# Additions by DMA held from the start, sums of x in five steps, and five raw weight buffers instead of six

## The chip, the cores and the metric

The kernel runs on one core of a Trainium2 chip. Its time is the device time of one execution in microseconds (us). A core has five engines with a queue of instructions each: PE (TensorE, matmuls; PEld is its weight load), DVE (VectorE), ACT (ScalarE), POOL (GpSimd) and SP (SyncE, which here only issues DMAs). Each engine runs its own queue in order.

## The reference

A bidirectional encoder trunk of two layers over x of 256 tokens by 1024, in float32, with FF = 2816:

```python
def rms_norm(x, g):
    return x * rsqrt(mean(x * x, axis=-1) + 1e-6) * g

def swiglu(h, w_gate, w_up, w_down):
    return (silu(h @ w_gate) * (h @ w_up)) @ w_down

for l in range(2):
    x = x + 0.5 * swiglu(rms_norm(x, ffn1_norm[l]), ffn1_w_gate[l], ffn1_w_up[l], ffn1_w_down[l])
    h = rms_norm(x, mix_norm[l])
    qa, ka, va, qb, kb, vb = split(h @ w_in[l])
    # windowed attention with sinks (a) and differential attention (b)
    x = x + concat(oA, oB) @ w_out[l]
    x = x + 0.5 * swiglu(rms_norm(x, ffn2_norm[l]), ffn2_w_gate[l], ffn2_w_up[l], ffn2_w_down[l])
out = rms_norm(x, final_norm)
```

The change touches the four FFNs (two in each layer) and the norm ahead of each. The attention between them is called mix below.

## The kernel before

**Weights.** All weights are read once from HBM, 200 MB in all, in steps of 1 MB: a step is a tile of 128 partitions with 8 KB each, called raw (N_RAW = 6 of them). To reach float32 accuracy, each raw half is split in two parts: ACT casts it to the matmul's type (the high half), DVE subtracts that from the raw values (the low half). Both lie in 4 KB tiles called w from the pool s4 (N_S4 = 28). A product takes three matmuls, high by high, low by high, high by low. The same is done with x and with the hidden part h, whose transposes on PE give hT.

**The planner.** `specs` is a list of Steps in the order of use. `weights()` takes the next step for PE and calls `ahead(n)`, which issues, up to a point n counted in half steps, the splits, the preparations of a step (`prep`) and the loads. n is `look[0]` half steps ahead of the step in use: IN_FFN = 8 in most FFNs, IN_MIX = 6 in the first FFN and in mix. `Split.part` calls `ahead` again when PE comes to the second half of a step. A load is issued when fewer than N_RAW raws are held; a raw is given back when its last split has been issued. The instructions stay in the order in which the program issues them on PE, ACT, DVE and POOL. Nothing is ordered by times.

**Groups.** An FFN goes through FF in five groups of 512 columns and a tail of 256. A group has gate and up products (x by 1024 rows of weights) and the down product of the group before, whose steps are down0 and down1 (two halves of the columns of D).

**Groups by seven** (`seven`, `by_seven`; the table SEVEN: groups 2 to 4 in the first FFN, 1 to 4 in the three others). Here the eight quarter products of a group's gate and up are replaced by seven, in the manner of a fast matrix multiplication, with sums of weights and sums of x. Four loads serve one group: a (gate, first half of the rows), b (up, first half), c (up, second half), d (gate, second half). Two sums of weights are formed by DMA: `gather(c, b)` reads c from HBM again and adds it onto b in SBUF, `gather(b, a)` adds b onto a. These are the additions of this document; POOL's queue issues them. Two more sums come from DVE: `plus(c, a)` and `plus(d, a)`, two instructions each, after which c, and then a and d, are free. From group 2 on, the steps in PE's order are: a, b+c, d, c, down0, a+b, a+b+c, a+b+c+d, down1. In group 1 of the later FFNs they are: a, d, down0, c, b+c, and then the same.

**Sums of x.** `make_sums` is a generator. It forms four combinations of the quarters of x with DVE, casts each on ACT and subtracts on DVE (three tiles with tag q and one with tag v). The FFN's code advances it by `next(sums)` at given points.

**Holding additions.** `issue` puts an addition on a list and lets it go at once, unless `hold` is set; `flush` clears `hold` and issues what has gathered, last in first out. Before, `hold` starts as False. `ffn_end` sets it, at the end of an FFN, and `Norm.stats` calls `flush` after it has computed r = (mean square + eps)^-0.5 on POOL. `stats` runs at the end of `take_x` (the first FFN's start) and in `Residual.late` (the others). In `take_x` it is followed by `constants()`, which puts ten or so small loads and operations for the attention on POOL's queue.

Of the kernel before, what the change touches and what calls it, by code (L numbers as in the profile page):

```python
# [12 lines left out]
ALU = mybir.AluOpType  # L13
# [8 lines left out]
NGRP = FF // 512  # L22
# [3 lines left out]
BIG = 1e33  # L26

AHEAD = 10
N_RAW, N_S4 = 6, 28
IN_FFN, IN_MIX = 8, 6  # L30
SEVEN = ((2, 3, 4), (1, 2, 3, 4))

# [2 lines left out]
def trunk(ctx: ExitStack, tc: tile.TileContext, x, n1, g1, u1, d1, nm, w_in, sink,  # L35
# [123 lines left out]
            issue(s.behind)  # L159


    pending, hold = [], [False]

    def issue(add):
        pending.append(add)
# [3 lines left out]
    def flush():  # L169
        hold[0] = False  # L170
        while pending:
            pending.pop(0)()
# [50 lines left out]
    look = [IN_MIX]  # L223
# [23 lines left out]
    def weights(less=0, held=False):  # L247

        i = at["use"]
        at["use"] += 1  # L250
        if i > 1:
            ahead(2 * i + look[0] - less)
        w = loaded[i]
        w.held = held
        return w
# [48 lines left out]
    class Norm:  # L304
# [42 lines left out]
        def make_sums(self):  # L347

            self.sm = []

            (t0, t1), (b0, b1) = [(t[:, :, 0:P], t[:, :, P:S]) for t in self.xg]

            def make(x, y, op):
                v = tmp().rearrange("p a (c s) -> p (a c) s", c=2)
                dve.tensor_tensor(v, x, y, op=op)
                tag, n = ("q", 3) if len(self.sm) < 3 else ("v", 1)
                sm = tp.tile([P, 2, 512], F32R, tag=tag, bufs=n, name=nm_(tag)).rearrange("p a (c s) -> p (a c) s", c=2)
                act.copy(sm[:, :, 0:P], v)
                self.sm.append(sm)
                return v  # L360

            def low(i, v):
                dve.tensor_tensor(self.sm[i][:, :, P:S], v, f(self.sm[i][:, :, 0:P]), op=ALU.subtract)

            s1 = make(b1, t1, ALU.subtract)
            s2 = make(s1, t0, ALU.add)
            low(0, s1)
            yield
            b0_ = make(b0, s2, ALU.subtract)
            low(1, s2)  # L370
            yield
            v = make(t1, t0, ALU.subtract)
            low(2, b0_)
            yield
            low(3, v)
            yield

# [10 lines left out]
        def stats(self, n=512):  # L388
            ms = tmp("ms", 2, (P, 2))
            dve.tensor_reduce(ms, self.ss.rearrange("p t (h q) -> p t h q", q=n // 256)[:, :, :, 0],  # L390
                              axis=mybir.AxisListType.X, op=ALU.add)
            dve.tensor_scalar(ms, ms, 1.0 / D, EPS, op0=ALU.mult, op1=ALU.add)
            self.r = tmp("r", 2, (P, 2))
            pool.tensor_tensor(self.r, ms, mhalf[:, 0:2], op=ALU.pow)
            flush()
            self.hr = tmp("hr", 2, (P, 2))
            dve.tensor_scalar_mul(self.hr, self.r, 0.5)

# [32 lines left out]
    def take_x(k):  # L431

        g, u = early
        if k == 0:
            for j in (0, 1):
                sl = norm.turn(j)
                next(g)
                norm.operands(j, sl)
                next(u)
        elif k == 1:  # L440
            for e in (g, u, g, u):
                next(e)
            norm.squares(0, 0, 512)
            norm.pair(2)
            norm.squares(1, 0, 512)
            ahead(5)
            norm.pair(3)
            norm.squares(0, 512, 512)
        elif k == 2:
            for e in early:  # L450
                next(e, None)
            ahead(7)
            norm.squares(1, 512, 512)
            norm.stats()
            constants()

    grow = const.tile([NG - 16, P], F32, name="grow")
    distB = const.tile([P, 2, S], F32, name="distB")
# [107 lines left out]
    class Residual:  # L566
# [14 lines left out]
        def late(self, k):  # L581

            if k == 1:
                self.nxt.pair(2)
                self.nxt.pair(3)
                self.squares(1)
            elif k == 2:
                self.nxt.stats()

    def ffn(norm, aside=None, before=None, final=False, sevens=SEVEN[1]):  # L590
        def silu(out_, acc, t):
# [3 lines left out]
        def gate(gs):  # L595
            g = []
            for t in range(2):
                n = gs[t].shape[1]
                g.append(silu(tmp().rearrange("p a n -> p (a n)")[:, :n], gs[t], t))
            return g  # L600
# [5 lines left out]
        def hidden(g, us):  # L606
            h = blk(F32)
            for t in range(2):
                up(h, us[t], g[t], t)
            return h  # L610

        def prod(xo, w):
            acc = bank()
            for k in range(4):
                hi, lo = w.part(k)
                xh, xl = xo(k)
                pe.matmul(acc, lhsT=xh, rhs=hi, start=k == 0, stop=False)
                pe.matmul(acc, lhsT=xl, rhs=hi, start=False, stop=False)
                pe.matmul(acc, lhsT=xh, rhs=lo, start=False, stop=k == 3)
            return acc  # L620

        def by_seven(h, g, sums):


            flat = lambda: tmp().rearrange("p a n -> p (a n)")

            def put(o, x, y, op):
                dve.tensor_tensor(o, x, y, op=op)
                return o

            m1, m7 = flat(), flat()
            if g > 1:
                act.copy(m1, prod(norm.quarter(0, 0), weights()))
                act.copy(m7, prod(norm.summed(3), weights(held=True)))
                hT = turn(h, 2)
                p2 = prod(norm.quarter(0, 1), weights())
                g0 = put(flat(), p2, m1, ALU.add)
                p3 = prod(norm.summed(2), weights())
                silu(g0, g0, 0)
                down(hT, g - 1, 0, weights())  # L640
            else:
                w = weights()
                next(sums, None)
                p1 = prod(norm.quarter(0, 0), w)
                hT = turn(h, (0,))
                w = weights()
                next(sums, None)
                act.copy(m1, p1)
                p2 = prod(norm.quarter(0, 1), w)
                hT += turn(h, (1,))  # L650
                w = weights()
                next(sums, None)
                g0 = put(flat(), p2, m1, ALU.add)
                silu(g0, g0, 0)
                down(hT, 0, 0, w)
                p3 = prod(norm.summed(2), weights())
                act.copy(m7, prod(norm.summed(3), weights()))
            h = blk(F32)
            p5 = prod(norm.summed(0), weights())
            late = g == max(sevens)  # L660
            p6 = prod(norm.summed(1), weights(look[0] - 5 if late else 0, late))
            u2 = put(flat(), p6, m1, ALU.subtract)
            u3 = put(m7, m7, u2, ALU.add)
            p4 = prod(norm.quarter(1, 1), weights(look[0] - 4 if late else 0, late))
            g1 = put(m1, p4, u3, ALU.subtract)
            w = weights(look[0] - 3 if late else 0)
            silu(g1, g1, 1)
            put(u3, u3, p5, ALU.subtract)
            put(u2, u2, p5, ALU.subtract)
            put(u2, u2, p3, ALU.add)  # L670
            up(h, u2, g0, 0)
            up(h, u3, g1, 1)
            down(hT, g - 1, 1, w)
            return h
# [19 lines left out]
        gs, us = [bank(), bank()], [bank(), bank()]  # L694
        if before is None:
            before = norm.late
        look[0] = IN_FFN - (1 in sevens)
        before(0)
        ws = (weights(), weights(2))
        for k in (0, 2):  # L700
# [7 lines left out]
        if 1 in sevens:  # L708
            norm.copies()
            sums = norm.make_sums()  # L710
        tokens(gs, norm.xs, w, 4)
        g = gate(gs)
        w = weights()
        next(sums, None)
        tokens(us, norm.xs, w, 4)
        h = hidden(g, us)
        for n in range(1, NGRP):
            if n in sevens:
                look[0] = IN_FFN + min(sevens) - n if before is not take_x else IN_MIX - (n == NGRP - 1)
                h = by_seven(h, n, sums)  # L720
                continue
            sums = norm.make_sums()
            gs = [bank(), bank()]
            tokens(gs, norm.xs, weights(), 0)
            hT = turn(h, 2)
            norm.copies()
            tokens(gs, norm.xs, weights(), 4)
            g = gate(gs)
            next(sums, None)
            us = [bank(), bank()]  # L730
            for k0 in (0, 4):
                tokens(us, norm.xs, weights(), k0)
                next(sums, None)
            h = hidden(g, us)
            for hh in range(2):
                down(hT, n - 1, hh, weights())
                if hh == 0:
                    next(sums, None)

        gu = [bank(), bank()]  # L740
        tokens(gu, norm.xs, weights(), 0)
# [390 lines left out]
```

## Time and profile before

| | us |
|---|---|
| median of 3 runs | 968.45 (966.74 to 970.66) |
| the profiled execution | 967.48 |
| its span in the trace | 965.7 |
| PE busy | 921.3 (95%) |
| DVE busy | 808.3 (84%) |
| ACT busy | 590.8 (61%) |
| POOL busy | 64.9 (7%) |

The FFNs' starts are at about 0, 316, 503 and 787 us (where the norm's r is made, or x is read). A row of a timeline reads: start, duration, engine, line, operation, output <- inputs, sizes, and how many like it were merged; in brackets stands the idle time before it, and what ended that. Nearly all instructions carry line 50, that of the helper that issues them, so they are told apart by their tiles. A row of the view by windows reads: the stretch and its length, then the busy time of PE, PEld, DVE, ACT and POOL with the number of instructions, the granted clock of PE, the DMA share and GB/s. A row of DMA issues ends with the median time from issue to landing.

### The profile page before, as it was taken

The page shows a single profiled execution, that of the slowest core. Times are in us where ns is not written, and L with a number is a line of the kernel's source. Part 1 is how long each engine was busy: PE and PEld are TensorE (multiplying, and loading weights), DVE is VectorE, ACT ScalarE, POOL GpSimd, SP SyncE. Part 2 cuts the span into 40 slices and gives each one's busy share as a digit, 9 for nine tenths or more (in the row PEclk, how much of TensorE's full clock was granted, in tenths as well). Part 3 has the DMA queues.
Part 4 walks back from the last instruction along what each step waited for, and adds up shares of the span by engine and source line. Part 5 has one row for each costly group of instructions (what it writes and reads, how often), then busy time and mean ns, then how long its engine had stood idle before and what let it go on. Part 6 is the DMA issues. An engine that isn't in the chain of part 4 may idle for free.

```text
span 965.7 us, 12600 instructions
## 1 busy us (share of the span) xinstructions
PE 921.3 (95%) x4696; PEld 771.9 (80%) x4696; DVE 808.3 (84%) x1125; ACT 590.8 (61%) x917; POOL 64.9 (7%) x83
## 2 busy tenths in 40 slices
PE   8499999999999889999997999999999996999997
PEld 6388888899888668888885888888998884888886
DVE  6376999959885699999868999997798668999995
ACT  7464766548765665665674675665577484666661
POOL 0220010000010110010010010000001010010011
PEclk9799999999999989999998999999999998999999
DMA  9893997947424786897748977978472357798841
GB/s 337 265 235 114 281 275 224 297 120 213 137 92 172 172 238 168 268 286 248 274 139 193 278 226 222 262 253 257 111 239 89 131 145 195 228 273 207 260 151 44
DMA packets 114061, 200.87 MB, mean 208 GB/s; under 512 B 3662, under 2 KB 31376, under 8 KB 114000
## 3 DMA queue, kind: packets, MB, share of 16 engines
q1 hardware_dynamic: 96528, 166.74, 50.5%
q0 software_dynamic: 16096, 31.75, 18.7%
q10 hardware_dynamic: 1376, 1.57, 0.5%
q8 instruction: 37, 0.61, 0.2%
q14 instruction: 24, 0.20, 0.1%
HBM read 199.00 MB, written 1.05 MB: 207 GB/s over the span
## 4 chain that ended last, share of the span: by engine, by line
PE 83%; DVE 7%; DMA 4%; ACT 3%; issue 1%; POOL 0%; SPq 0%; ACTq 0%; POOLq 0%; DVEq 0%
PE ps L50 83%; DVE w L50 4%; ACT w L50 2%; DMA raw<-in_ffn_w_up_dram 1%; DMA raw<-in_ffn_w_gate_dram 1%; DVE tmp L50 1%; DVE s L50 1%; DVE raw L50 1%; DMA xk<-in_x_dram 1%; ACT tmp L50 1%; ACT L50 0%; ACT q L50 0%; ACT v L50 0%; POOL raw L50 0%; SPq L153 0%
## 5 line engine op out<-in xcount | busy, mean ns | idle before, releaser
L50 PE MATMUL ps<-w,s 128*128 128x512 f32 (+1 forms) x2574 | 614.2, 396 | 30.9 <-ACT tmp L50 13.1
L50 PEld LDWEIGHTS ps<-w,s 128*128 128x128 f32 x2574 | 484.5, 191 | 136.2 <-ACT tmp L50 14.3
L50 DVE TENSOR_TENSOR w<-raw,w 128x1024 fp32r<-128x1024 f32 (+1 forms) x458 | 484.0, 1100 | 56.3 <-ACT w L50 54.3
L50 ACT CAST w<-raw 128x1024 fp32r<-128x1024 f32 (+1 forms) x458 | 409.6, 952 | 102.9 <-DVE raw L50 86.2
L50 PE MATMUL ps<-w,q 128*128 128x512 f32 x540 | 127.7, 390 | 0.0
L50 PEld LDWEIGHTS ps<-w,q 128*128 128x128 f32 x540 | 101.9, 189 | 21.4
L50 PE MATMUL ps<-s,w 128*128 128x256 f32 x672 | 84.0, 285 | 0.0
L50 PEld LDWEIGHTS ps<-s,w 128*128 128x128 f32 x672 | 81.7, 192 | 1.1
L50 DVE TENSOR_TENSOR raw<-raw,raw 128x1024 f32<-128x1024 f32 x60 | 70.6, 1217 | 0.0
L50 POOL DMA_DIRECT2D raw<-in_ffn_w_up_dram x30 | 39.1, 1357 | 409.8 <-DVE w L50 138.2
L50 ACT ACTIVATE s<-ps,gcol 128x256 fp32r<-128x256 f32 (+1 forms) x80 | 31.4, 479 | 46.6 <-PE ps L50 45.0
L50 ACT ACTIVATE tmp<-tmp,r 128x512 f32<-128x512 f32 x30 | 21.7, 723 | 49.4 <-DVE tmp L50 49.4
L50 PE MATMUL ps<-ident,s 128*128 128x128 f32 x304 | 41.2, 274 | 2.7 <-DVE s L50 2.7
L50 PE MATMUL ps<-w,v 128*128 128x512 f32 x180 | 43.3, 389 | 0.0
L50 PEld LDWEIGHTS ps<-ident,s 128*128 128x128 f32 x304 | 35.1, 140 | 9.8 <-ACT w L50 2.9
L50 PEld LDWEIGHTS ps<-w,v 128*128 128x128 f32 x180 | 33.8, 188 | 7.0
L50 ACT COPY tmp<-ps 128x512 f32<-128x512 f32 x34 | 19.9, 585 | 31.8 <-PE ps L50 29.4
L50 ACT ACTIVATE s<-s,negm 128x256 f32<-128x256 f32 x64 | 31.9, 500 | 6.6 <-DVE negm L50 6.4
L50 DVE TENSOR_TENSOR s<-ps,s 128x512 fp32r<-128x512 f32 x44 | 28.7, 683 | 7.9 <-ACT s L50 7.9
L50 ACT CAST s<-ps 128x512 fp32r<-128x512 f32 x44 | 24.2, 592 | 18.1 <-PE ps L50 18.1
L50 DVE TENSOR_TENSOR tmp<-ps,tmp 128x512 f32<-128x512 f32 x49 | 33.4, 682 | 1.6 <-PE ps L50 1.6
L50 ACT CAST q<-tmp 128x512 fp32r<-128x512 f32 x20 | 12.4, 621 | 34.7 <-DVE tmp L50 34.3
(106 smaller groups left out, 417.6 us busy)
## 6 DMA issues: line engine op xcount, KB each, us to landing
raw<-in_ffn_w_down_dram SPq DMA_DIRECT2D x44, 1024.0 KB, 6.4
raw<-in_ffn_w_gate_dram SPq DMA_DIRECT2D x39, 1024.0 KB, 8.6
raw<-in_ffn_w_up_dram SPq DMA_DIRECT2D x39, 1024.0 KB, 5.1
raw<-in_ffn_w_up_dram POOLq DMA_DIRECT2D x30, 1024.0 KB, 10.3
raw<-in_w_in_dram SPq DMA_DIRECT2D x14, 1024.0 KB, 5.6
raw<-in_ffn_w_gate_dram SPq DMA_DIRECT2D x8, 512.0 KB, 6.7
raw<-in_ffn_w_up_dram SPq DMA_DIRECT2D x8, 512.0 KB, 7.6
raw<-in_w_in_dram SPq DMA_DIRECT2D x8, 512.0 KB, 5.7
```

The lines of the kernel that those rows point to most:

```text
L50: ins = issue(*a, **k)
```

## The change

Three things are changed together. Additions by DMA are held from the beginning of the program, and `flush` is called by the callers of `stats`: in `take_x` behind `constants()`, in `Residual.late` right behind `stats`. `make_sums` yields after each group of DVE additions and after each group of casts, five times instead of four, with two casts in one step, and the places of its `next` calls move with it. The raw buffers are five instead of six, and the 8 KB go to two more tiles of the pool s4, with which the splits in FFNs that begin with a group by seven run one half step further ahead. In group 1 of these FFNs the `weights()` calls stand at slightly other places.

```diff
@@ -26,7 +26,7 @@
 BIG = 1e33
 
 AHEAD = 10
-N_RAW, N_S4 = 6, 28
+N_RAW, N_S4 = 5, 30
 IN_FFN, IN_MIX = 8, 6
 SEVEN = ((2, 3, 4), (1, 2, 3, 4))
 
@@ -159,7 +159,7 @@
             issue(s.behind)
 
 
-    pending, hold = [], [False]
+    pending, hold = [], [True]
 
     def issue(add):
         pending.append(add)
@@ -350,28 +350,35 @@
 
             (t0, t1), (b0, b1) = [(t[:, :, 0:P], t[:, :, P:S]) for t in self.xg]
 
-            def make(x, y, op):
+            def add(x, y, op):
                 v = tmp().rearrange("p a (c s) -> p (a c) s", c=2)
                 dve.tensor_tensor(v, x, y, op=op)
+                return v
+
+            def high(v):
                 tag, n = ("q", 3) if len(self.sm) < 3 else ("v", 1)
                 sm = tp.tile([P, 2, 512], F32R, tag=tag, bufs=n, name=nm_(tag)).rearrange("p a (c s) -> p (a c) s", c=2)
                 act.copy(sm[:, :, 0:P], v)
                 self.sm.append(sm)
-                return v
 
             def low(i, v):
                 dve.tensor_tensor(self.sm[i][:, :, P:S], v, f(self.sm[i][:, :, 0:P]), op=ALU.subtract)
 
-            s1 = make(b1, t1, ALU.subtract)
-            s2 = make(s1, t0, ALU.add)
+            s1 = add(b1, t1, ALU.subtract)
+            s2 = add(s1, t0, ALU.add)
+            yield
+            high(s1)
+            high(s2)
+            yield
             low(0, s1)
+            b0_ = add(b0, s2, ALU.subtract)
+            low(1, s2)
+            v = add(t1, t0, ALU.subtract)
             yield
-            b0_ = make(b0, s2, ALU.subtract)
-            low(1, s2)
+            high(b0_)
+            high(v)
             yield
-            v = make(t1, t0, ALU.subtract)
             low(2, b0_)
-            yield
             low(3, v)
             yield
 
@@ -392,7 +399,6 @@
             dve.tensor_scalar(ms, ms, 1.0 / D, EPS, op0=ALU.mult, op1=ALU.add)
             self.r = tmp("r", 2, (P, 2))
             pool.tensor_tensor(self.r, ms, mhalf[:, 0:2], op=ALU.pow)
-            flush()
             self.hr = tmp("hr", 2, (P, 2))
             dve.tensor_scalar_mul(self.hr, self.r, 0.5)
 
@@ -453,6 +459,7 @@
             norm.squares(1, 512, 512)
             norm.stats()
             constants()
+            flush()
 
     grow = const.tile([NG - 16, P], F32, name="grow")
     distB = const.tile([P, 2, S], F32, name="distB")
@@ -586,6 +593,7 @@
                 self.squares(1)
             elif k == 2:
                 self.nxt.stats()
+                flush()
 
     def ffn(norm, aside=None, before=None, final=False, sevens=SEVEN[1]):
         def silu(out_, acc, t):
@@ -639,17 +647,15 @@
                 silu(g0, g0, 0)
                 down(hT, g - 1, 0, weights())
             else:
+                p1 = prod(norm.quarter(0, 0), weights())
+                hT = turn(h, (0,))
+                next(sums, None)
                 w = weights()
-                next(sums, None)
-                p1 = prod(norm.quarter(0, 0), w)
-                hT = turn(h, (0,))
-                w = weights()
-                next(sums, None)
                 act.copy(m1, p1)
                 p2 = prod(norm.quarter(0, 1), w)
                 hT += turn(h, (1,))
+                next(sums, None)
                 w = weights()
-                next(sums, None)
                 g0 = put(flat(), p2, m1, ALU.add)
                 silu(g0, g0, 0)
                 down(hT, 0, 0, w)
@@ -694,7 +700,7 @@
         gs, us = [bank(), bank()], [bank(), bank()]
         if before is None:
             before = norm.late
-        look[0] = IN_FFN - (1 in sevens)
+        look[0] = IN_FFN
         before(0)
         ws = (weights(), weights(2))
         for k in (0, 2):
@@ -708,15 +714,21 @@
         if 1 in sevens:
             norm.copies()
             sums = norm.make_sums()
+            next(sums)
         tokens(gs, norm.xs, w, 4)
-        g = gate(gs)
-        w = weights()
+        if 1 in sevens:
+            w = weights()
+            g = gate(gs)
+        else:
+            g = gate(gs)
+            w = weights()
         next(sums, None)
         tokens(us, norm.xs, w, 4)
         h = hidden(g, us)
+        next(sums, None)
         for n in range(1, NGRP):
             if n in sevens:
-                look[0] = IN_FFN + min(sevens) - n if before is not take_x else IN_MIX - (n == NGRP - 1)
+                look[0] = IN_FFN + 1 + min(sevens) - n if before is not take_x else IN_MIX - (n == NGRP - 1)
                 h = by_seven(h, n, sums)
                 continue
             sums = norm.make_sums()
@@ -734,8 +746,7 @@
             h = hidden(g, us)
             for hh in range(2):
                 down(hT, n - 1, hh, weights())
-                if hh == 0:
-                    next(sums, None)
+                next(sums, None)
 
         gu = [bank(), bank()]
         tokens(gu, norm.xs, weights(), 0)
```

## The prediction

> **What bounds the kernel now.** I read the page's busy line first, then the windows by stage, then the timelines of single engines at the places that the change touches.
>
> ```profile
> PE 921.3 (95%) x4696; PEld 771.9 (80%) x4696; DVE 808.3 (84%) x1125; ACT 590.8 (61%) x917; POOL 64.9 (7%) x83
> ...
> 87.00:165.00 78.00, 77.56 (x351) 64.05 (x349) 77.13 (x80) 49.80 (x57) 5.14 (x4) 1.00 0.85 244
> 345.00:450.00 105.00, 105.00 (x470) 87.00 (x470) 100.50 (x103) 65.97 (x76) 6.42 (x5) 0.99 0.84 245
> 317.00:343.00 26.00, 19.42 (x77) 14.62 (x76) 19.30 (x22) 14.87 (x19) 2.56 (x2) 0.90 0.74 170
> ```
>
> Over the span PE is the bound, at 95%. But in the groups by seven (87 to 165 in the first FFN, 345 to 450 in the second) DVE is full too: 77.13 of 78.00 us and 100.50 of 105.00. The third line is the start of the second FFN, where neither is full. The end of the groups shows how much PE still lies behind DVE:
>
> ```profile
> 449.91 3.57 DVE L50 TENSOR_TENSOR w<-raw,w 128x1024 fp32r<-128x1024 f32 x3
> 450.94 2.24 PE L50 MATMUL ps<-w,s 128*128 128x512 f32 x9
> 164.91 3.47 PE L50 MATMUL ps<-w,s 128*128 128x512 f32 x14 [0.44 <-DVE w L50]
> ```
>
> The first of DVE's three low halves ends at about 451.1. PE's nine matmuls begin at 450.94, and the third of them, some 0.5 us later, is the first that takes that half. So the reserve there is 0.3 us, and at 164.91 PE already waits 0.44 for DVE. **What DVE loses inside the groups by seven, PE loses at their end.** The idle time of PE is at the start and in the three later FFN starts, shown below.
>
> **Part 1: the start.** Additions are held from the beginning and let go behind the constants. Before, the first addition stands ahead of r (the norm's reciprocal root) on POOL's queue.
>
> ```profile
> 27.20 0.17 DVE L50 TENSOR_SCALAR ms<-ms 128x2 f32<-128x2 f32 x1
> 29.43 1.28 ACT L50 ACT_TABLE_LOAD   x1
> 41.42 1.48 POOL L50 DMA_DIRECT2D raw<-in_ffn_w_up_dram  x1 [39.91 <-DMA raw<-in_ffn_w_up_dram]
> 42.43 1.25 POOL L50 TENSOR_TENSOR r<-ms,mhalf 128x2 f32<-128x2 f32 x1
> 43.71 1.27 ACT L50 ACTIVATE tmp<-ps,r 128x512 f32<-128x512 f32 x2 [12.99 <-POOL r L50]
> 44.45 7.14 PE L50 MATMUL ps<-w,s 128*128 128x512 f32 x24 [13.13 <-ACT tmp L50]
> 127.57 5.60 PE L50 MATMUL ps<-w,q 128*128 128x512 f32 x24
> ```
>
> The mean square is ready at 27.37, and r could follow at once (it lasts 1.25). POOL instead waits for the load that the addition adds onto, and makes r at 42.43. ACT's table load ends at 30.71 and silu needs some 0.7 more for PE's first bank, so PE can go on at 31.45, not 44.45: 13.0 us. PE's next 24 matmuls took 7.14 us, against 5.60 for 24 at 127.57; without the stall I take these 1.5 us back as well. Sum: −14.5.
>
> The addition now waits behind the constants on POOL, whose own waits for DMAs move with it:
>
> ```profile
> 59.82 0.50 POOL L50 TENSOR_TENSOR s<-s 128x128 f32<-128x128 f32 x1 [3.25 <-DMA s<-in_lam_k_dram]
> 84.96 1.04 PE L50 MATMUL ps<-ident,s 128*128 128x128 f32 x8
> ```
>
> From the end of r (43.68) to the end of the constants (60.32) pass 16.6 us before. After, r ends at about 28.7, so the constants end by 45.3, and the first addition lands by 45.3 + 11.3 = 56.6 (its time is priced below). DVE meets the sum's split ahead of the hidden part that PE transposes at 84.96, which is due at 84.96 − 14.5 = 70.5. With a pair of splits (2.35, as at 106.86), h and the small sums between, which I take as 4 us, it must be there at about 64. That is 7 us of cover, so I cost it at nothing; beyond it each us costs one.
>
> **Part 2: five raw buffers.** One buffer less makes each load wait for a later release. For mix, tails and down steps the loads land 7 us or more ahead of their first read, and a shift of one release costs nothing. One chain has no such room. In a group by seven, b of the next group is loaded, c is added onto it by a DMA on POOL's queue, and ACT and DVE split the sum.
>
> ```profile
> 89.00 0.37 SPq L153 DMA_DIRECT2D raw<-in_ffn_w_up_dram  x1
> 91.16 2.35 DVE L50 TENSOR_TENSOR raw<-raw,raw 128x1024 f32<-128x1024 f32 x2
> 94.61 1.29 POOL L50 DMA_DIRECT2D raw<-in_ffn_w_up_dram  x1 [28.06 <-DVE tmp L50]
> 106.86 2.35 DVE L50 TENSOR_TENSOR w<-raw,w 128x1024 fp32r<-128x1024 f32 x2
> ...
> 372.34 0.37 SPq L153 DMA_DIRECT2D raw<-in_ffn_w_up_dram  x1
> 377.07 2.35 DVE L50 TENSOR_TENSOR raw<-raw,raw 128x1024 f32<-128x1024 f32 x2
> 378.00 1.29 POOL L50 DMA_DIRECT2D raw<-in_ffn_w_up_dram  x1 [19.29 <-DMA raw<-in_ffn_w_up_dram]
> 386.19 6.90 DVE L50 TENSOR_TENSOR w<-raw,w 128x1024 fp32r<-128x1024 f32 x6 [0.34 <-ACT w L50]
> 409.72 2.35 DVE L50 TENSOR_TENSOR raw<-raw,raw 128x1024 f32<-128x1024 f32 x2
> 425.41 2.35 DVE L50 TENSOR_TENSOR w<-raw,w 128x1024 fp32r<-128x1024 f32 x2
> ```
>
> Before, the load of b starts at 89.00 and 372.34, as soon as the split of a down step has freed the sixth buffer. With five, that split frees a buffer that an earlier load already claims, and b waits for the next release, of c, by DVE's second addition: 91.16 + 2.35 = 93.51 in the first FFN, 379.42 and 412.07 in the second. DVE has a fixed amount of work from there to the first half of the sum: 106.86 − 93.51 = 13.35 us; 391.87 (the sixth of the x6 at 386.19) − 379.42 = 12.45; 425.41 − 412.07 = 13.3, of which two additions of tmp, 0.6 each, now stand behind it, 12.1. Against it stands the chain:
>
> ```profile
> raw<-in_ffn_w_up_dram SPq DMA_DIRECT2D x9, 1024.0 KB, 5.1
> raw<-in_ffn_w_up_dram POOLq DMA_DIRECT2D x7, 1024.0 KB, 10.3
> ...
> raw<-in_ffn_w_up_dram POOLq DMA_DIRECT2D x4, 1024.0 KB, 11.3
> ...
> raw<-in_ffn_w_up_dram POOLq DMA_DIRECT2D x1, 1024.0 KB, 8.3
> ...
> 24.60 1.05 ACT L50 CAST w<-raw 128x1024 fp32r<-128x1024 f32 x1
> ```
>
> The load takes 5.1, POOL issues 0.6 after it (378.00 against 372.34 + 5.1), the addition takes 10.3 among the second and third FFN's loads (first two lines), 11.3 in the first FFN's groups, 8.3 for the one with the least beside it, and ACT's cast 1.05. I take 10.3, since in these groups other loads go on beside it: 5.1 + 0.6 + 10.3 + 1.05 = 17.05. DVE waits 17.05 − 13.35 = 3.7 in each of the two loops of the first FFN, and 4.6 and 5.0 in each later FFN. The turn from group 1 to 2 there is about neutral: the first group's order leaves more between. On DVE everything behind the split stands in order behind the wait: low halves, h, the next release, and so PE's matmuls. The ends: with 8.3 each of the eight waits is 2.0 shorter, −16 in all; with 11.3 each is 1.0 longer, +8.
>
> The Trainium skill ("DMA: Bandwidth & Descriptors", section "Anatomy of one DMA — SWDGE (gpsimd) path") fits a transfer on this queue by 2.0 us plus the bytes over 436 GB/s; an estimate from it is 4.4 us for 1 MB, which would make the loop 11.2 us, and no wait. The trace does not agree: its shortest such addition here is 8.3, so the measurement decides.
>
> **Part 3: the three later FFN starts.** After, the second addition is let go with the first by one flush, as before, but the sums of x come in five steps, and the split runs half a step earlier.
>
> ```profile
> 315.63 2.65 POOL L50 DMA_DIRECT2D raw<-in_ffn_w_up_dram  x2
> raw<-in_ffn_w_up_dram POOLq DMA_DIRECT2D x2, 1024.0 KB, 10.9
> 334.48 4.81 PE L50 MATMUL ps<-w,s 128*128 128x512 f32 x12 [0.88 <-DVE s L50]
> 342.43 5.06 PE L50 MATMUL ps<-w,s 128*128 128x512 f32 x11 [3.14 <-DVE s L50]
> 503.44 2.67 POOL L50 DMA_DIRECT2D raw<-in_ffn_w_up_dram  x2 [0.21 <-issue]
> 528.77 4.36 PE L50 MATMUL ps<-w,s 128*128 128x512 f32 x11 [3.07 <-DVE s L50]
> 787.33 2.65 POOL L50 DMA_DIRECT2D raw<-in_ffn_w_up_dram  x2 [0.21 <-issue]
> 813.89 5.06 PE L50 MATMUL ps<-w,s 128*128 128x512 f32 x11 [3.14 <-DVE s L50]
> 373.35 1.29 DVE L50 TENSOR_TENSOR s<-ps,s 128x512 fp32r<-128x512 f32 x2 [1.04 <-ACT s L50]
> ```
>
> The two additions issued at 315.63 take 10.9 in the mean, so with 8.3 for the first the second takes 13.5 and lands at about 329.9. After, the split of that sum (a + b) stands ahead of the first hT on ACT and DVE, and the small sums behind it. From 329.9: cast 1.05, low half 1.2, s 0.6, low half 1.2 behind the next cast (at 334.8), two additions 2.35, low half 1.2, s 0.65: PE goes on at 339.0, not 342.43, a gain of 3.4; 2.7 if ACT adds its two casts of sums. From POOL's issue to PE's start that makes 23.4 us; before they are 26.8, 25.3 and 26.6, so the third FFN gains 1.5 less and the fourth 0.2 less. Of the 3.4, DVE brings 3.0 to the sum of group 2, and its wait of 1.04 (last line) goes: −4.1. If the new stalls pull the clock down as the idle time before 334.48 seems to (12 matmuls in 4.81 us, with a granted clock of 0.90 in 317 to 343), each FFN may lose up to 2.
>
> On that the Trainium skill ("TensorE: Matmul & The Clock Gate", Part 1) has TensorE fall to half speed only after a whole idle window, about 3.4 us long; by it the stalls of Part 2, spread over several waits, would cost nothing more. The row at 334.48 speaks against it, since the waits just before were short (0.88); I keep the 2 us as an upper end only.
>
> **The sum**, against the profiled execution (967.48, span 965.7; 1.0 under the median of 968.45). First FFN: −14.5 + 3.7 + 3.7 + 0.1 = −7.0. Second: −4.1 + 4.6 + 5.0 − 0.2 of PE's reserve = +5.3. Third: +6.8. Fourth: +5.5. Total **+10.6: 978.1 for that execution, 979.0 at the median**. With 11.3 for the additions 987, with 8.3 963.
>
> **Rivals.** *The loop is hidden (faster).* If b's load starts as early as before, or the chain takes no more than the 12.1 to 13.35 us of DVE's work, the eight waits vanish, and what stays is −14.5 − 4.1 − 2.6 − 3.9 = −25.1: 943. It decides at an addition of about 5.4 to 6.6 us. Against it stands the shortest in the trace, 8.3; for it, only that five buffers leave less traffic beside an addition. Chance 0.14. This is also where the 4.4 us of the Trainium skill would lead.
>
> *Additions run as if alone.* Fewer loads in flight, 8.3 for all: +10.6 − 16 = −5.4, 963. For it: loads after b wait for a release too, so some additions start alone. Against: the next release comes 2 to 5 us later. Chance 0.12.
>
> *The start pays less.* The constants wait for their own DMAs, and if waits like the 3.25 at 59.82 come to 10 us more in all, or the additions crowd, the sum of group 2 lands 3 us and more after 64 and PE waits for h there as much: 984 to 988 with 5 to 9 us of the 14.5 gone. Chance 0.12.
>
> *The hold does nothing* cannot be: in the built order r stands ahead of both additions on POOL.
>
> **How the numbers follow.** The forecast has 0.62, own range 972 to 987. The range of 962 to 990 leaves out the first rival (0.14) and some 0.06 of the others' edges. About 0.5% (4.8 us) is what a measurement of this kernel tells from no change: faster is under 963.6, slower over 973.3. Faster: 0.14 + 0.05 of the second rival = 0.19. Same: 0.07 of the second rival and 0.05 of the forecast's low edge = 0.12. Slower: 0.57 + 0.12 = 0.69.
>
> **What would show it.** After: PE idle near 31 us under 1.5, r before any addition on POOL; b's load at the end of DVE's second addition in groups 2 and 3; an ACT or DVE wait of 3 to 5 us on the addition ahead of the sum's split, eight times; PE idle for DVE by about as much in groups 3 and 4; PE's restart in the later FFNs 23 to 24 us after POOL's issue. Wrong if DVE does not wait there, or the additions take under 7 us.

## The result: 4.5% slower, and the profile after

The changed kernel takes 1011.6 us in the median (1011.01 to 1012.73), against 968.27 for the kernel before on the same chip: 1.0447 times, interval 1.0423 to 1.0470, +43.3 us. The forecast was 979.0 within 962 to 990: the sign was right, the size four times too small. The profiled execution has a span of 1009.2 us, 43.5 over the one before.

The chain that ended last by engine, before:

```profile
PE 83%; DVE 7%; DMA 4%; ACT 3%; issue 1%; POOL 0%; SPq 0%; ACTq 0%; POOLq 0%; DVEq 0%
```

The page of the changed kernel: the busy line, the chain that ended last by engine, and the additions among the DMA issues (the last column is the median time from issue to landing).

```profile
PE 940.2 (93%) x4696; PEld 781.0 (77%) x4696; DVE 806.4 (80%) x1125; ACT 588.6 (58%) x917; POOL 69.0 (7%) x83
...
PE 50%; DMA 19%; DVE 17%; issue 9%; ACT 5%; POOL 0%; POOLq 0%; ACTq 0%; DVEq 0%
...
raw<-in_ffn_w_up_dram POOLq DMA_DIRECT2D x30, 1024.0 KB, 13.1
```

DVE and ACT have no more work than before (806.4 for 808.3, 588.6 for 590.8), and PE's 19 us more are the same matmuls at a lower clock (0.964 granted in the mean, for 0.979). But DMA now holds 19% of the chain, against 4%, and an addition takes 13.1 us in the median of all 30, against 10.3. The same stretch of the second FFN that was full before, by windows:

```profile
345.00:450.00 105.00, 92.50 (x394) 74.08 (x392) 83.99 (x88) 56.42 (x65) 7.70 (x6) 0.97 0.80 223
```

DVE is busy for 83.99 of 105 us instead of 100.50, and PE for 92.50 instead of 105.00: both now wait. Where the time went is read from PE, whose order of work the change leaves almost as it was, so that the same matmul can be found in both traces:

| the same matmul | before | after | shift | this step, measured | forecast |
|---|---|---|---|---|---|
| behind the start's stall | 47.54 | 32.12 | −15.4 | −15.4 | −14.5 |
| end of the first FFN | 167.08 | 169.51 | +2.4 | +17.8 | +7.5 |
| second FFN, group 1 | 348.24 | 346.74 | −1.5 | −3.9 | −4.1 |
| its end | 467.06 | 483.93 | +16.9 | +18.4 | +9.4 |
| third FFN, group 1 | 541.83 | 557.08 | +15.2 | −1.6 | −2.6 |
| its end | 648.02 | 678.94 | +30.9 | +15.7 | +9.4 |
| fourth FFN, group 1 | 828.81 | 856.03 | +27.2 | −3.7 | −3.9 |
| its end | 947.14 | 990.67 | +43.5 | +16.3 | +9.4 |

All four gains came within 1 us of the forecast. All four losses in the groups by seven came 6 to 10 us too high; that is the whole miss (10.3 + 9.0 + 6.3 + 6.9 = 32.5).

**The start.** Timelines of PE, POOL, ACT and DVE, changed kernel:

```profile
24.63 11.52 PE L50 MATMUL ps<-w,s 128*128 128x512 f32 x50
27.45 0.72 POOL L50 TENSOR_TENSOR r<-ms,mhalf 128x2 f32<-128x2 f32 x1 [25.95 <-DVE ms L50]
43.23 1.38 POOL L50 DMA_DIRECT2D raw<-in_ffn_w_up_dram  x1 [2.69 <-DVE w L50]
57.12 3.90 ACT L50 CAST w<-raw 128x1024 fp32r<-128x1024 f32 x4 [10.53 <-DMA raw<-in_ffn_w_up_dram]
58.20 2.36 DVE L50 TENSOR_TENSOR w<-raw,w 128x1024 fp32r<-128x1024 f32 x2 [10.65 <-ACT w L50]
69.35 0.68 DVE L50 TENSOR_TENSOR v<-tmp,v 128x512 fp32r<-128x512 f32 x1
70.09 4.38 PE L50 MATMUL ps<-w,v 128*128 128x512 f32 x11 [2.91 <-DVE v L50]
```

PE runs through the place where it stood for 13.1 us. The two additions that were held, onto b and then onto a, go in the order in which they were gathered: `flush` takes the first of the list (`pending.pop(0)`), not the last. Then ACT waits 10.5 us for the first addition, and DVE behind it, and a sum of x (v) that stands behind them in DVE's order comes 2.9 us late for PE.

**The loop.** The second FFN, changed kernel, SP, POOL, ACT, DVE and PE in order of time:

```profile
341.52 0.37 SPq L153 DMA_DIRECT2D raw<-in_ffn_w_up_dram  x1
347.33 1.28 POOL L50 DMA_DIRECT2D raw<-in_ffn_w_up_dram  x1 [26.66 <-DVE raw L50]
347.93 0.37 SPq L153 DMA_DIRECT2D raw<-in_ffn_w_gate_dram  x1
361.11 3.90 ACT L50 CAST w<-raw 128x1024 fp32r<-128x1024 f32 x4 [5.62 <-DMA raw<-in_ffn_w_up_dram]
...
380.04 2.35 DVE L50 TENSOR_TENSOR raw<-raw,raw 128x1024 f32<-128x1024 f32 x2
382.42 0.37 SPq L153 DMA_DIRECT2D raw<-in_ffn_w_up_dram  x1
387.83 1.28 POOL L50 DMA_DIRECT2D raw<-in_ffn_w_up_dram  x1 [29.06 <-DVE tmp L50]
399.81 4.83 ACT L50 CAST w<-raw 128x1024 fp32r<-128x1024 f32 x5 [7.31 <-DMA raw<-in_ffn_w_up_dram]
400.89 2.36 DVE L50 TENSOR_TENSOR w<-raw,w 128x1024 fp32r<-128x1024 f32 x2 [6.47 <-ACT w L50]
404.00 4.58 PE L50 MATMUL ps<-w,s 128*128 128x512 f32 x12 [4.06 <-DVE tmp L50]
...
439.63 2.94 ACT L50 CAST w<-raw 128x1024 fp32r<-128x1024 f32 x3 [8.01 <-DMA raw<-in_ffn_w_up_dram]
442.68 4.53 PE L50 MATMUL ps<-w,s 128*128 128x512 f32 x12 [5.18 <-ACT w L50]
```

It is the loop that the prediction drew: DVE's second addition ends at 382.39, b's load goes at 382.42, POOL issues the addition at 387.83, and ACT, which has waited 7.31 us, reads the sum at 399.81; DVE waits 6.47 and PE 4.06. The corresponding places before:

```profile
333.86 0.37 SPq L153 DMA_DIRECT2D raw<-in_ffn_w_up_dram  x1
339.42 1.28 POOL L50 DMA_DIRECT2D raw<-in_ffn_w_up_dram  x1 [21.14 <-DMA raw<-in_ffn_w_up_dram]
353.69 4.84 ACT L50 CAST w<-raw 128x1024 fp32r<-128x1024 f32 x5
385.12 7.68 ACT L50 CAST w<-raw 128x1024 fp32r<-128x1024 f32 x8
423.50 2.96 ACT L50 CAST w<-raw 128x1024 fp32r<-128x1024 f32 x3 [1.32 <-DMA raw<-in_ffn_w_up_dram]
```

There ACT read the sums at 355.6 (the third of the x5), 389.9 (the sixth of the x8) and 423.50. So it reads them 5.5, 9.9 and 16.1 us later after the change. 16.1 of PE's 16.9 at this FFN's end are there already, and the chain that ended last has no matmul between 363 and 450. Over the whole kernel, the view of waits (us in total, times, longest) has this before, and this after:

```profile
ACT w L50 <- DMA raw<-in_ffn_w_up_dram: 11.2, 10, 2.3
```

```profile
ACT w L50 <- DMA raw<-in_ffn_w_up_dram: 109.3, 19, 10.5
```

### The profile page after: what moved, and what is told of

Same layout as the page of the kernel before. It is cut to its first block, busy times and chain, and to the rows that moved or that the text cites. A ratio compares the mean times of both kernels' runs of the same rounds, so it can differ in the third digit from the quotient of the medians.

```text
span 1009.2 us, 12603 instructions
## 1 busy us (share of the span) xinstructions
PE 940.2 (93%) x4696; PEld 781.0 (77%) x4696; DVE 806.4 (80%) x1125; ACT 588.6 (58%) x917; POOL 69.0 (7%) x83
## 4 chain that ended last, share of the span: by engine, by line
PE 50%; DMA 19%; DVE 17%; issue 9%; ACT 5%; POOL 0%; POOLq 0%; ACTq 0%; DVEq 0%
PE ps L50 50%; DMA raw<-in_ffn_w_up_dram 19%; DVE w L50 9%; ACT w L50 3%; DVE raw L50 3%; DVE tmp L50 2%; DVE s L50 2%; ACT s L50 1%; ACT junk L50 0%; DMA xk<-in_x_dram 0%; POOL rb L50 0%; ACT q L50 0%; ACT v L50 0%; DVE xk L50 0%; DVE q L50 0%
## 5 line engine op out<-in xcount | busy, mean ns | idle before, releaser
L50 PE MATMUL ps<-w,s 128*128 128x512 f32 (+1 forms) x2574 | 623.1, 400 | 41.0 <-ACT w L50 14.7
L50 PE MATMUL ps<-w,v 128*128 128x512 f32 x180 | 51.0, 438 | 13.1 <-DVE tmp L50 10.2
L50 PEld LDWEIGHTS ps<-w,v 128*128 128x128 f32 x180 | 38.7, 218 | 24.4 <-issue 12.2
L50 DVE TENSOR_TENSOR tmp<-tmp,ps 128x512 f32<-128x512 f32 x45 | 29.4, 681 | 0.5
L50 DVE SCALAR_TENSOR_TENSOR s<-ps,gcol,s 128x256 fp32r<-128x256 f32 x48 | 20.3, 477 | 11.2 <-ACT s L50 11.1
## 6 DMA issues: line engine op xcount, KB each, us to landing
raw<-in_ffn_w_up_dram POOLq DMA_DIRECT2D x30, 1024.0 KB, 13.1
```

The lines of the kernel that those rows point to most:

```text
L50: ins = issue(*a, **k)
```

## The experiments

All times are medians against the kernel before on the same chip (967.7 to 968.6 us).

| kernel | held | sums | raws | half step | b ahead of a | us | ratio (95%) |
|---|---|---|---|---|---|---|---|
| changed kernel | yes | five | 5 | yes | no | 1011.6 | 1.0447 (1.0423–1.0470) |
| e3_hold | yes | four | 6 | no | no | 952.1 | 0.9838 (0.9823–0.9853) |
| e5_sums | no | five | 6 | no | no | 957.7 | 0.9889 (0.9871–0.9908) |
| e12_five_alone | no | four | 5 | no | no | 1007.8 | 1.0405 (1.0385–1.0425) |
| e2_five_raw | no | four | 5 | yes | no | 1011.5 | 1.0442 (1.0413–1.0471) |
| e1_six_raw | yes | five | 6 | no | no | 946.1 | 0.9773 (0.9731–0.9815) |
| e6_six_raw_look_after | yes | five | 6 | yes | no | 955.4 | 0.9870 (0.9852–0.9887) |
| e4_five_raw_look_before | yes | five | 5 | no | no | 999.2 | 1.0322 (1.0296–1.0347) |
| e7_b_before_a | yes | five | 5 | yes | yes | 949.7 | 0.9814 (0.9792–0.9835) |
| e10_five_b_before_a_look | yes | five | 5 | no | yes | 942.5 | 0.9729 (0.9706–0.9751) |
| e9_six_b_before_a | yes | five | 6 | no | yes | 942.8 | 0.9735 (0.9717–0.9753) |
| e11_hold_b_before_a | yes | four | 6 | no | yes | 953.2 | 0.9841 (0.9822–0.9859) |
| e8_loads_wait | yes | five | 5 | yes | no | 1039.2 | 1.0745 (1.0717–1.0772) |

**The parts alone.** e3 takes the hold alone, e5 the sums alone, e2 the buffers with the half step; e1 is the change without the buffers and the half step:

```diff
-N_RAW, N_S4 = 5, 30
+N_RAW, N_S4 = 6, 28
-        look[0] = IN_FFN
+        look[0] = IN_FFN - (1 in sevens)
-                look[0] = IN_FFN + 1 + min(sevens) - n if ...
+                look[0] = IN_FFN + min(sevens) - n if ...
```

> The kernel before with only the first part: additions held from the start and let go behind the constants, and right behind the norm's statistics in the later FFNs. Theory A: PE's 13.1 us of idle time at the start go and its next matmuls run at full clock: 950 to 956 us, nothing changed later. Rival C (letting both additions go later costs elsewhere what the start gains): 962 us or more.

> The kernel before with only the second part: sums of x in five steps, with the calls moved as in the change. Theory A: the three later FFN starts gain 1 to 3 us each at most: 960 to 968 us. Rival B: 985 us or more, with DVE waits in the groups by seven.

> The changed kernel with six raw buffers, 28 tiles of 4 KB and the splits as far ahead as before; additions held from the start and sums of x in five steps stay. Theory A (the loss is the loop of five buffers: b's load waits for DVE's second addition, and the addition by DMA onto b, 13.1 us in the mean of the changed kernel, ends 0.1 us before ACT reads it in every group): the loop is hidden again, additions onto b take about 10 us, and the start's 15 us stay gained: 943 to 955 us. Rival B (the new order of the sums of x and of the splits causes the loss, by its place on ACT and DVE): 985 to 1010 us.

> The kernel before with only the third part: five raw buffers, 30 tiles of 4 KB, splits half a step further ahead. Theory A: no gain at the start, and 11 loops that each cost PE 5 to 6 us, less what the turn from group 1 to 2 hides: 1015 to 1030 us, with additions onto b of about 13 us. Rival B: 965 to 985 us.

The hold alone gains 16.1 us, as A said. The sums alone gain 10.5, 2 more than A's best. Both together gain 22.1 with six buffers, so rivals B and C fall: neither new order is the loss by itself. The buffers with the half step give the whole 1011.5 by themselves, below A's 1015, because A took the start's stall to remain there. It doesn't, as the cleanest cut shows.

**Five buffers and nothing else.**

```diff
-N_RAW, N_S4 = 6, 28
+N_RAW, N_S4 = 5, 28
```

> The kernel before with five raw buffers instead of six and nothing else. Theory A: b's load waits for DVE's second addition as in the changed kernel, about 50 us in 11 loops, less 14.6 us at the start, where the later load of b puts the first addition behind r without any hold: 995 to 1008 us. Rival J (the loss comes only from five buffers and the half step together): 955 to 980 us.

1007.8: one number of one line costs 39 us net. Its start, PE and POOL:

```profile
23.80 12.64 PE L50 MATMUL ps<-w,s 128*128 128x512 f32 x55
...
27.23 0.72 POOL L50 TENSOR_TENSOR r<-ms,mhalf 128x2 f32<-128x2 f32 x1 [25.73 <-DVE ms L50]
```

With five buffers b's load itself is issued later, so the first addition falls behind r on POOL without any hold, and PE starts the table's first matmul 15.1 us earlier than before. This is one reason why the parts do not add: in the changed kernel the hold gains nothing that the fifth buffer would not have brought. The other is that the gain of the sums is lost too. Read by the table's matmuls in the profiled executions, the changed kernel gains 4.6, 4.7 and 3.9 us over e2 at the three later FFN starts, and loses 4.8, 5.7, 3.4 and 4.1 to it in the four FFNs behind. With six buffers (e1 against e3) the starts gain 4.6, 2.9 and 4.3, and only the first FFN loses 4.7; the others lose 0.4 at most.

**Buffers or half step.** e4 undoes only the half step, e6 only the buffers.

> The changed kernel with the splits only as far ahead as before (half a step less); five raw buffers, 30 tiles of 4 KB, held additions and sums in five steps stay. Theory A (the number of raw buffers alone makes the loop): 1000 to 1020 us, and ACT reads each sum b+c 0.1 us after its addition has landed. Rival D (running the splits half a step further ahead makes the loop): 945 to 975 us.

> The changed kernel with six raw buffers and 28 tiles of 4 KB, splits half a step further ahead as in the change. Theory A: 940 to 955 us, as with the splits half a step later. Rival D: 985 us or more.

The number of buffers (six with 28 tiles of s4 against five with 30) is worth 53.1 us without the half step (946.1 to 999.2) and 56.2 with it (955.4 to 1011.6). Theory A holds, both times under 1 us past an end of its range, since the half step, which it took as free, costs 12.4 with five buffers and 9.3 with six (with the old sums, e12 to e2, 3.7). One place of it is seen in the turn from group 1 to 2 of the second FFN in e4 (SP, POOL, ACT):

```profile
337.84 0.37 SPq L153 DMA_DIRECT2D raw<-in_ffn_w_up_dram  x1
343.58 1.28 POOL L50 DMA_DIRECT2D raw<-in_ffn_w_up_dram  x1 [24.60 <-ACT w L50]
346.94 0.37 SPq L153 DMA_DIRECT2D raw<-in_ffn_w_gate_dram  x1
353.78 3.96 ACT L50 CAST w<-raw 128x1024 fp32r<-128x1024 f32 x4 [1.50 <-DMA raw<-in_ffn_w_up_dram]
```

Here the next load starts 3.4 us behind POOL's issue, and the addition takes 10.1 us (343.58 to the read at 353.78, less 0.1). With the half step it starts 0.6 behind (347.93 against 347.33), and the addition takes 13.7; ACT waits 5.62 instead of 1.50. Why the releases come closer together there, and what the half step costs with six buffers, was not taken apart.

**The loop cut at its head.** If the loop is the cause, b must only take an earlier release. In groups 2 to 4 the order of two loads is exchanged; the order of use stays:

```diff
+    def turned(i):
+        return i + (i in swapped) - (i - 1 in swapped)
...
-                    for _ in emit_dma(at["dma"]):
+                    for _ in emit_dma(turned(at["dma"])):
```

> The changed kernel, five raw buffers, with the order of two loads exchanged in groups 2 to 4 of every FFN: b of the next group is loaded ahead of its a. Theory A: b's load starts at the release that a's load had, the split of down0, 4.5 us earlier, and with it the addition; the 11 loops shorten by 4.5 us each, and a, which is read some 8 us after it lands, takes the later place without a wait: 950 to 975 us. Rival E (the addition ends late because its queue or the loads are full, whenever b comes): 1000 us or more.

949.7, 62 us under the changed kernel with the same five buffers, and a little under A's range. In its second FFN:

```profile
357.48 0.37 SPq L154 DMA_DIRECT2D raw<-in_ffn_w_up_dram  x1
360.83 2.35 DVE L50 TENSOR_TENSOR raw<-raw,raw 128x1024 f32<-128x1024 f32 x2
375.37 3.90 ACT L50 CAST w<-raw 128x1024 fp32r<-128x1024 f32 x4 [2.06 <-DMA raw<-in_ffn_w_up_dram]
```

b's load now goes 5.7 us ahead of the end of DVE's second addition (363.18), and ACT's wait at this turn is 2.06, not 7.31. Rival E falls. The addition itself is no shorter: POOL issues it at 362.99 and it lands at 375.27, 12.3 us against 11.9 in the changed kernel (the eleven between groups take 11.2 in the mean, against 12.4). So it is the earlier start that brings the gain.

**What makes the addition long.** A transfer of 4 bytes from b on SP's queue holds the loads behind b until the addition has landed (`kept_sp` is SP's queue by the helper that keeps the program's order; the loads go by it too, and what that alone costs was not run):

```diff
             issue(s.behind)
+            if not hold[0]:
+                kept_sp.dma_start(fence, raw[0:1, 0, 0:1])
...
```

> The changed kernel, five raw buffers, with a transfer of 4 bytes from b on SP's queue behind b's load, which waits for the addition onto b: the loads behind b start only when the addition has landed. Theory G (the addition takes 12.8 us and not 8.3 because of the three loads beside it): additions onto b of 8.3 to 9.0 us, each loop 4 us shorter, 965 to 995 us, the upper half if the loads held back come late in their turn. Rival F (it is slow for its own sake, by its place on POOL's queue): additions of 12 us or more, and 1011 us or more.

The additions onto b take 8.3 to 8.6 us in ten of the eleven turns of this kernel (10.0 in the other): G holds for the duration, F falls. But the time is 1039.2, far above G's 965 to 995. SP and ACT in the second FFN:

```profile
392.09 0.37 SPq L50 DMA_DIRECT2D raw<-in_ffn_w_up_dram  x1
405.96 0.61 SPq L50 DMA_DIRECT2D fence<-raw  x1
406.66 0.99 SPq L50 DMA_DIRECT2D raw<-in_ffn_w_gate_dram  x1
...
406.05 2.00 ACT L50 CAST w<-raw 128x1024 fp32r<-128x1024 f32 x2 [3.86 <-DMA raw<-in_ffn_w_up_dram]
415.74 1.99 ACT L50 CAST w<-raw 128x1024 fp32r<-128x1024 f32 x2 [7.70 <-DMA raw<-in_ffn_w_gate_dram]
```

The wait for b+c shrinks to 3.86, and the load of the next weights, which had run beside the addition, comes 7.70 us late in its place. A shorter addition bought with idle loads is worth nothing here.

**Better versions.**

> Six raw buffers and splits as far ahead as before, held additions, sums in five steps, and b of the next group loaded ahead of its a in groups 2 to 4. Theory A (what is left of the loop is the addition landing 0.1 us before ACT's read at the turns 2 to 3 and 3 to 4, and an earlier b takes that away): 935 to 946 us. Rival H (DVE's own work, 106 of 110 us, bounds these groups, so that an earlier addition brings nothing): 944 to 950 us.

> Five raw buffers with b loaded ahead of a, held additions, sums in five steps, and splits only as far ahead as before. Theory A with the half step as a cost of its own (9 to 12 us in the two pairs run so far): 936 to 945 us. Rival I (the half step costs only where the loop is tight, and here it is not): 947 to 952 us, as with the half step.

> The kernel before with held additions and with b loaded ahead of a; sums of x in four steps as before, six raw buffers. Theory A: 940 to 952 us. Rival H: 950 to 954 us, as with held additions alone.

e9 and e10, with held additions, sums in five steps, b ahead of a and no half step, take 942.8 and 942.5 us: 2.7% under the kernel before, with six buffers or with five. Both lie in A's range; in e10 the half step is worth 7.2 us against e7, so rival I falls. In e9 the addition now lands some 9.5 us ahead of ACT's read at the turn from group 2 to 3 of the second FFN (362.75 for 372.20), where in e1 it was 0.1 (377.22 for 377.32). But that this gains time with six buffers is not shown: the four runs of e1 go from 942.4 to 950.9, around e9's 942.8. With the old sums (e11, 953.2) the earlier b brings nothing over e3, as H said; in e3's trace the groups of the later FFNs already take as long as before, within 0.1 us by the table's matmuls, so there was no loss to take back.

## Why the prediction was right in sign and wrong in size

- **What bounds the groups: right.** "What DVE loses inside the groups by seven, PE loses at their end" holds: 16.1 us at ACT's read, 16.9 at PE.
- **Part 1's gain: right** (15.4 for 14.5). The constants were no obstacle: POOL issues the first addition at 43.23 and it lands at 57.0, where 56.6 was the forecast's late end; that they agree is luck, since the addition took 13.8 us instead of 11.3 and was issued 2.1 earlier. **Its cover: wrong.** I named h as what is due behind the sum's split and put it at 64. What was due first is a sum of x, v, which the new steps of the sums place behind that split. With the hold alone, where the old order stands, its low half is in time (PE, e3):

```profile
67.30 2.95 PE L50 MATMUL ps<-w,v 128*128 128x512 f32 x12
```

  There is no wait, and twelve matmuls take 2.95 us. In the changed kernel eleven take 4.38 behind 2.91 of idle time: 4.6 us together. The step that failed is "I cost it at nothing": the change's own second part moved another instruction behind the wait. PE waits for v here, by 1.0 to 3.7 us, in all eight kernels that have both the hold and the five steps, and in none of the others.
- **Part 2's loop: right in place, release and condition**; e12 and e7 show it from both sides. **Its price: wrong at two terms.** First, "the addition takes 10.3". Between 345 and 470 of the changed kernel, and in e8 with the loads held (345 to 500):

```profile
raw<-in_ffn_w_up_dram POOLq DMA_DIRECT2D x6, 1024.0 KB, 13.1
...
raw<-in_ffn_w_up_dram POOLq DMA_DIRECT2D x6, 1024.0 KB, 9.4
```

  These medians, like the forecast's 10.3 and 11.3, mix additions onto a and onto b. Onto b alone, which the loop holds, the eleven between groups took 9.1 to 11.3 us before (9.9 in the mean), 10.4 to 13.7 after (12.4) and 8.3 to 10.0 in e8 (8.6). I had noted that other loads go on beside the addition, but took the duration of a kernel in which the addition started ahead of the releases that follow. Delaying b put it right into them. My bounds, 8.3 to 11.3, were all rows of the undelayed state, so the upper end was too low. In the first FFN, ACT reads the sums of groups 3 and 4 at these times before and after:

```profile
104.89 2.95 ACT L50 CAST w<-raw 128x1024 fp32r<-128x1024 f32 x3 [1.27 <-DMA raw<-in_ffn_w_up_dram]
137.27 2.95 ACT L50 CAST w<-raw 128x1024 fp32r<-128x1024 f32 x3 [1.44 <-DMA raw<-in_ffn_w_up_dram]
```

```profile
101.74 2.94 ACT L50 CAST w<-raw 128x1024 fp32r<-128x1024 f32 x3 [8.82 <-DMA raw<-in_ffn_w_up_dram]
140.48 2.94 ACT L50 CAST w<-raw 128x1024 fp32r<-128x1024 f32 x3 [8.69 <-DMA raw<-in_ffn_w_up_dram]
```

  From the one to the other pass 38.7 us instead of 32.4: this turn loses 6.4, where I had 3.7. The turn before it loses more: from the start's −15.4 to the −3.1 of the first of these reads are 12.3 us, 4.6 of them v's.
- Second, and worth more: **"the turn from group 1 to 2 there is about neutral".** The rows show b's load 7.7 us later (341.52 for 333.86) and the addition 4.5 longer (13.7 for the 9.2 of before), 12.2 us against a slack of 7.0 (it had landed at 348.6 and was read at 355.6). The sum is read 5.5 us later; I had it 4.1 earlier than before, relative to the FFN's entry, where it came 3.1 later (5.5 − 2.4). That is 7.2 us in this FFN (3.1 + 4.1), and by the same working 5.9 and 5.7 in the third and fourth, where ACT reads this sum at 541.6 and 826.9 before (the third of each group of casts), and after at 561.83 and 859.62, with entries of +16.9 and +30.9:

```profile
539.75 4.85 ACT L50 CAST w<-raw 128x1024 fp32r<-128x1024 f32 x5
824.96 5.80 ACT L50 CAST w<-raw 128x1024 fp32r<-128x1024 f32 x6
```

```profile
561.83 4.84 ACT L50 CAST w<-raw 128x1024 fp32r<-128x1024 f32 x5 [4.10 <-DMA raw<-in_ffn_w_up_dram]
859.62 4.85 ACT L50 CAST w<-raw 128x1024 fp32r<-128x1024 f32 x5 [4.04 <-DMA raw<-in_ffn_w_up_dram]
```

  I worked out the chain for two turns and waved the third through. These 18.8 us, v's 4.6 and some 9 in the two later turns make up the 32.5. In the three later FFNs those two turns lose 29.3 us where I had 28.8, but that is luck: in e4, where the first turn loses less, they lose 36.7.
- **The half step: priced at nothing, costs 9 to 12 us** (e4, e6). I looked only at which splits it moves, not at how it moves the releases that start loads. With five buffers this is in the main the loss of the turn from group 1 to 2 over again, not a further one. Without the half step (e4) ACT reads this sum 2.5, 1.6 and 3.0 us earlier than before, relative to the FFN's entry, against 4.1, 2.6 and 3.9 forecast; with it 3.1, 3.3 and 1.8 later. With the half step and the old sums (e2) it is read 0.2 earlier, 1.5 later and 0.6 earlier: there the turn is neutral, as forecast. So what failed is the sum of two terms, a gain of the new sums that reaches group 2 and a half step that costs nothing.
- **Part 3: right in size.** PE goes on in three pieces:

```profile
336.04 0.50 PE L50 MATMUL ps<-w,s 128*128 128x512 f32 x1 [3.42 <-ACT s L50]
337.41 5.49 PE L50 MATMUL ps<-w,s 128*128 128x512 f32 x12 [0.87 <-DVE s L50]
343.35 2.87 PE L50 MATMUL ps<-w,s 128*128 128x512 f32 x11 [0.46 <-DVE s L50]
```

  Not at 339.0 in one stroke, and the last piece starts 25.3 us after POOL's issue (318.02) instead of 23 to 24, but the three FFN starts gain 3.9, 1.6 and 3.7 for 4.1, 2.6 and 3.9.
- **Additions as if alone** decided nothing: e8 shows that their speed and the loads' lateness are one account. **The loop is hidden** is what e7 makes of it, by another order. The row at 404.00 (4.58 us for twelve matmuls behind 4.06 of idle time, against the 2.95 of e3 without a wait) shows the slow clock behind a stall once more (0.76 granted from 404 to 411); since DVE's chain already makes 16.1 of the 16.9 us, it adds at most 0.8 here. Against the rule of the Trainium skill ("TensorE: Matmul & The Clock Gate", Part 1), a stall of 2.91 us, under its window of about 3.4, was followed by slow matmuls too (70.09), with a granted clock of 0.57 from 70 to 74. The length of a stall alone does not decide it here: in e8 PE stands 2.89 us at the same place, up to 70.49, and the granted clock from 70 to 74 is 1.00.

## What to carry to other kernels

When a buffer goes, find for each load which release it waits for now, and work the chain behind it out for every turn, not for the typical one. A transfer that is delayed does not keep its duration: look at what is released next to it, and take the price from the busiest such place or widen the bound. Before buying a buffer back, try which of two loads takes the earlier release: here that order was worth 62 us with the five buffers and made the sixth unnecessary.

## What the runs showed of the hardware

The same 1 MB addition by DMA onto b took 8.3 to 8.6 us in ten of eleven cases with the loads behind it held, and 10.4 to 13.7 between the groups of the changed kernel, where three 1 MB loads run beside it on another queue. Holding the loads made it fast again, and the kernel slower.
